# Buffers, marks and begin times in the recurrence of a hybrid block, and four weight loads of its branch stage

## The chip, the cores and the metric

One core of one Trainium2 chip. The metric is the device time of one execution in microseconds. The engines named below are TensorE (PE, with its weight loads PEld), VectorE (DVE), ScalarE (ACT), GpSimd (POOL), and the SyncE queue (SP), which issues most DMAs.

## The reference

One block over 1024 tokens of 1024 channels, all in float32: an input norm and one wide projection, attention with a forget gate (8 heads of 64), an RWKV-7 recurrence (8 heads of 64), a gated sum of the two, an output projection, and a feed-forward net with a short convolution. The change lies in the recurrence and in the gated sum:

```python
def step(state, inp):
    r_t, w_t, k_t, v_t, a_t, b_t = inp
    sa = jnp.einsum('bhvk,bhk->bhv', state, a_t)
    state = state * w_t[:, :, None, :] + sa[..., None] * b_t[:, :, None, :] \
            + v_t[..., None] * k_t[:, :, None, :]
    return state, jnp.einsum('bhvk,bhk->bhv', state, r_t)
...
bonus = (jnp.sum(r_h * k_h * r_k, axis=-1, keepdims=True) * v_h).reshape(bsz, seq, RWKV_WIDTH)
return ((y + bonus) * g).astype(p.dtype)
...
merged = gate_fox * (o_fox @ fox_w_out) + gate_rwkv * (o_rwkv @ rwkv_w_out)
return merged @ w_o
```

## The kernel before

Products with weights are made from split operands: a float32 tile becomes a high part (`hi`) and a rest (`lo`), and three matmuls give one product. The cast to `hi` is done by ACT, the subtraction for `lo` by DVE (L274).

The recurrence runs in chunks of 64 tokens. Its work is cut into eight units, k = 0 to 7: four pairs of heads `p`, each in two halves `hf` of 512 tokens; names such as `cum1_0` or `X0_1` end in p_hf, so `cum1_0` is unit 2. Each unit has a preparation, `pre`, and a main chain, `main`. Three streams are woven together on PE in an order written when the program is built: the main chain of one unit, the preparation of a later one, and as filling the matmuls of the projections (`qk`, `rkv`, `v`, the gates `gt`). The weaver keeps a clock of its own (`weave.now`, in ns) from the costs of the matmuls; a step that yields a number lets that much of filling pass. PE's order is fixed so; on the other engines a scheduler places the instructions, and each engine and each DMA queue works in its order.

The steps that matter here:

- `pre` loads the decay `cum` (L711) and the gains `al` (L713) by SP, scans `cum` on DVE (L715), and ACT makes `el` (L719) and `en` (L721) from it. L732 to L744 form `kr`, `ar`, `bk` and again `al`. PE multiplies `ar` and `bk` into `p`, L764 takes it from PSUM into `E`.
- Corner blocks of `E` go by a store (`sm`, L772) and a load (`M`, L776) into 32-row form; 31 pairs of small DVE operations (L784, L786) invert them; a store and a load (L797) bring the result into `TT`.
- `head_sums` makes the bonus sum `bs`: it splits its operand into two tiles, multiplies both by a block matrix, and L827 uses the sum.
- `main` transposes corners of `TT` into `X` (L842, two instructions), and from `X` come `xi`, `zi`, `TT` again (L859 on ACT) and `uw` on PE, then the chunk states and `y`.
- Tiles of the pool `rw` have one buffer where nothing else is said (`cum`, `al`, `el`, `en`, `kr`), so a load into one waits for the last reader of what is in it.
- A mark with NOSYNC orders two instructions of the same engine without a wait: the one comes behind the other in the queue. L842 has such marks behind the last `S` and the last `E`.
- `ready` (L777) is the time at which a unit's main chain begins, on the weaver's clock. 
- `shifted` empties the bank of a projection: ACT writes `sh` (L366), DVE the result (L369; the `v` of it is the last of a unit). `qk_steps` empties by L393 on ACT and L395 on DVE, and stores both parts with DMAs into `d_st`.

In the branch stage, `br_load` loads the weights of the two gated products, x = 0 for attention and x = 1 for the recurrence, n = 0 to 7, through a tile `raw` with two buffers; ACT casts them (L1219), POOL makes the rest (L1222), and `br_open` loads the gate `g` (L1224). `after_gate` puts an instruction behind the last load of a `g` on SP.

Of the kernel before, what the change touches and what calls it, by code (L numbers as in the profile page):

```python
# [10 lines left out]
F32R = mybir.dt.float32r  # L11
AF = mybir.ActivationFunctionType
ALU = mybir.AluOpType
# [3 lines left out]
S = 1024  # L17
KT = 8
NH = 512
# [113 lines left out]
def hybrid_block(ctx: ExitStack, tc: tile.TileContext, a, out):  # L133
    nc = tc.nc
    weave = Weave()
    ctx.enter_context(tc.manual_schedule(engines={mybir.EngineType.PE}))

    def mm(o, lhsT, rhs, start, stop, more=False):

        weave.mm_cost(o, lhsT, rhs)  # L140
        nc.tensor.matmul(o, lhsT, rhs, start=start, stop=stop, skip_group_check=more)  # L141
# [5 lines left out]
    def f32(ap):  # L147
        return ap.bitcast(F32)

    tt, stt, ts = nc.vector.tensor_tensor, nc.vector.scalar_tensor_tensor, nc.vector.tensor_scalar  # L150
# [15 lines left out]
    def V(name, i=0, n=1):  # L166
        o, _ = VEC[name]
        return vec[:, o + i : o + i + n]
# [13 lines left out]
    omu = cp.tile([128, 14], F32, name="omu")  # L182
# [61 lines left out]
    marks = {}  # L244
# [40 lines left out]
    def gemm_steps(ps, w, x, cs, nk=KT, w0=0, by_kt=False):  # L285
        (wh, wl), (xh, xl) = w, x
        order = [(i, kt) for i in range(3) for kt in range(nk)]
        if by_kt:
            order.sort(key=lambda o: o[1])
        for n, (i, kt) in enumerate(order):  # L290
            ww, xx = ((wh, xh), (wh, xl), (wl, xh))[i]
            k0 = (w0 + kt) * 128
            mm(ps, ww[:, k0 : k0 + 128], xx[:, kt, cs], start=n == 0, stop=n == len(order) - 1)
            yield
# [51 lines left out]
    with ExitStack() as es:  # L346
# [4 lines left out]
        def big(name):  # L351
            return pb.tile([128, NH], F32, tag="big", name=name)

        def gen(name):
            return pr.tile([128, NH], F32, tag="gen", name=name)

        def shifted(w, ti, hf, dst, prev, name, by_kt=False):

            ps = big(f"ps_{name}{hf}")
            yield from gemm_steps(ps, w, u, slice(hf * NH, hf * NH + NH), by_kt=by_kt)  # L360
            sh = shp.tile([128, NH + 1], F32, tag="sh", name=f"sh_{name}{hf}")
            if hf == 0:
                nc.vector.memset(sh[:, 0:1], 0.0)
            else:
                nc.vector.tensor_copy(sh[:, 0:1], prev)
            nc.scalar.activation(sh[:, 1 : NH + 1], ps, AF.Copy, scale=V("mu", ti))  # L366
            if hf == 0:
                nc.gpsimd.tensor_copy(prev, sh[:, NH : NH + 1])
            stt(dst, ps, omu[:, ti : ti + 1], sh[:, 0:NH], op0=ALU.mult, op1=ALU.add)  # L369

        rkv, got, last_col = {}, {}, {}

# [28 lines left out]
        HS = (slice(0, 64), slice(64, 128))  # L401
# [11 lines left out]
        with tc.tile_pool(name="st", bufs=1) as st, tc.tile_pool(name="stp", bufs=2, space=PS) as stp, \  # L413
# [126 lines left out]
            for half in range(2):  # L540
                for kt in u_steps(half):
                    low_part(kt, half, (0, 1))
                    if half == 0 and kt in (3, 5):
                        raw, hi, lo = low_raw[kt == 5]
# [145 lines left out]
        def head_sums(ps, x, hi, lo):  # L690

            nc.scalar.copy(hi, x)
            nc.gpsimd.tensor_tensor(lo, x, f32(hi), op=ALU.subtract)
            yield 3400
            mm(ps, blk_r, hi, start=True, stop=False)
            mm(ps, blk_r, lo, start=False, stop=True)

        def pre(k, p, hf):

            n = f"{p}_{hf}"  # L700
# [3 lines left out]
            def tmp(nm, w=NH, bufs=1, dt=F32):  # L704
                return rw.tile([128, w], dt, tag=nm, name=f"{nm}{n}", bufs=bufs)

            def chunk_tile(nm, bufs, *dims):
                return rw.tile([128, *dims], F32, tag=nm, name=f"{nm}{n}", bufs=bufs)

            cum = tmp("cum")  # L710
            nc.sync.dma_start(cum, d_lora[0, p, :, cs])  # L711
            al = tmp("al")
            nc.sync.dma_start(al, d_lora[1, p, :, cs])  # L713
            for c0 in (0, 256):
                nc.vector.tensor_tensor_scan(cum[:, c0 : c0 + 256], cst2[:, 128:384], cum[:, c0 : c0 + 256], initial=0.0,  # L715
                                             op0=ALU.mult, op1=ALU.add)
# [3 lines left out]
            en = tmp("en")  # L720
# [10 lines left out]
            kr = tmp("kr")  # L731
# [15 lines left out]
            rkb = tmp("ksq")  # L747
# [6 lines left out]
            E = chunk_tile("E", 2, NCU, 2, 3, CH)  # L754
            QA = chunk_tile("QA", 2, NCU, 2, CH)
            UV = chunk_tile("UV", 2, NCU, 2, CH)
            for c0 in range(0, NCU, 4):
                ps = [gen(f"p1_{n}{h}{c0}") for h in range(2)]
# [15 lines left out]
            M32 = chunk_tile("M32", 1, 32, 32)  # L774
            for g in range(4):
                nc.sync.dma_start(M32[g * 32 : g * 32 + 32, :, :], sm.rearrange("h c b s t -> (h c b) s t"))  # L776
            ready = weave.now + (49500 if k == 0 else 38500)  # L777
            E32 = chunk_tile("E32", 1, 8, 32)
            nc.gpsimd.dma_start(E32, a["cst"][:, CST["einit"][0] :].rearrange("p (j t) -> p j t", t=32))
            t32 = tmp("t32", 128)  # L780
# [26 lines left out]
            a4 = at.rearrange("p (b h s) -> p b h s", h=2, s=CH)  # L807
            for e in range(2):
                for h in range(2):
                    nc.scalar.copy(UV[HS[1 - h], e::2, h, :], v4[HS[e], :, h, :])  # L810
                    nc.vector.tensor_copy(QA[HS[h], e::2, 1, :], a4[HS[e], :, h, :])
            yield 2000
            ps = [gen(f"tb{n}{h}") for h in range(2)]
            for c in range(NCU):
# [7 lines left out]
                    mm(q[HS[h], c * CH : c * CH + CH], E[HS[1 - h], c, h, 0, :], UV[HS[1 - h], c, h, :], start=True, stop=True)  # L822
            nc.vector.tensor_copy(QA[:, :, 0, :], c3(q))
            bp = gen(f"bs{n}")
            yield from head_sums(bp, rkb, tmp("cum", dt=F32R), tmp("en", dt=F32R))
            bon = tmp("bon", bufs=2)
            tt(bon, bp, vv, op=ALU.mult)  # L827
            units[p, hf] = dict(ready=ready, pcd=pcd, ar=ar, E=E, QA=QA, TT=TT, bon=bon, UV=UV)
# [1 line left out]
        def main(k, p, hf):  # L830
            o = units.pop((p, hf))
            n = f"{p}_{hf}"
            cs = slice(hf * NH, hf * NH + NH)
            pcd, ar, E, QA, TT, bon, UV = (o[k] for k in ("pcd", "ar", "E", "QA", "TT", "bon", "UV"))
# [5 lines left out]
            yield max(0, o["ready"] - weave.now - 2500)  # L840
            for h in range(2):
                i = nc.vector.transpose(X[B0[h], :, :], TT[B0[h], :, 0:32])  # L842
                for x in ("S", "E"):
                    if x in marks:
                        tc.add_manual_dep(i.ins, marks[x].ins.name, NOSYNC)
            yield max(1300, o["ready"] - weave.now)
# [16 lines left out]
            for c0 in range(0, NCU, 4):  # L863
                ps = gen(f"uw{n}{c0}")
                for c in range(c0, c0 + 4):
                    for h in range(2):
                        x = (c - c0) * 128
# [7 lines left out]
            for c0 in range(0, NCU, 4):  # L875
                ps = gen(f"mz{n}{c0}")
                for c in range(c0, c0 + 4):
                    for h in range(2):
                        x = (c - c0) * 128
# [9 lines left out]
            S = [state.get(p)]  # L889
# [85 lines left out]
        def main_chain():  # L975
            for k, (p, hf) in enumerate(order):
                while (p, hf) not in units:
                    yield 200
                yield from main(k, p, hf)
                yield 0  # L980
# [205 lines left out]
    def bank(k, name):  # L1186
        return pb.tile([128, NH], F32, tag="big", name=name) if k > 5 else pz.tile([128, NH], F32, tag=f"p{k}", name=name)
# [16 lines left out]
    def after_gate(i):  # L1204
        if "g" in marks:
            tc.add_manual_dep(i.ins, marks["g"].ins.name, NOSYNC)

    def br_load(x, n):
        raw = br_raw[x, n] = rp.tile([128, 1024], F32, tag="raw", name=f"raw_br{x}{n}")[:, 0:NH]
        after_gate(nc.sync.dma_start(raw, a["w_br"][n, :, x * NH : x * NH + NH]))  # L1210

    def br_open(x, n):
        if (x, n) not in br_raw:
# [15 lines left out]
    if "rest" in marks:  # L1229
        g, m = (gsp.tile([128, NH], F32, tag="sp0", name=f"rest{k}") for k in range(2))  # L1230
        i = nc.scalar.activation(g, marks["rest"], AF.Abs)
# [89 lines left out]
    for x in range(2):  # L1321
        for n in range(8):
            if x or n:
                k = 8 * x + n + 1
# [320 lines left out]
    ps = {t: [bank(k, f"wo{t}_{c}") for c, k in enumerate(ks)] for t, ks in enumerate(((0, 5), (6, 7), (1, 2)))}  # L1645
# [13 lines left out]
    def wo_do(t, k):  # L1659
        ps = [bank(k + c, f"wo{t}_{c}") for c in range(2)]  # L1660
        for kt in range(KT):
            wo_mm(t, kt, ps)
        return ps

    ps = wo_do(3, 3)
# [7 lines left out]
    ps = wo_do(4, 0)  # L1673
# [15 lines left out]
    for t, k in ((5, 2), (6, 6), (7, 4)):  # L1689
        ps = wo_do(t, k)  # L1690
# [234 lines left out]
    for s, k in enumerate(ORDER):  # L1925
        ps = banks[4:] if k in (7, 4, 2) else banks[0:4]
# [109 lines left out]
```

## Time and profile before

Three runs: median 1654.64 us (1653.51 to 1662.36). The profiled execution took 1657.87 us, its span is 1656.1 us, the mean granted clock of TensorE 0.994. From the profile, by stage (us busy):

| stage | from, to | length | PE | DVE | ACT | POOL | granted clock |
|---|---|---|---|---|---|---|---|
| norm, small projections | 0 to 140 | 140.0 | 127.05 | 98.49 | 76.33 | 12.06 | 0.98 |
| recurrence with projections | 140 to 620 | 480.0 | 467.39 | 344.32 | 231.67 | 62.18 | 1.00 |
| attention | 620 to 827 | 207.0 | 198.81 | 163.81 | 137.21 | 35.40 | 0.99 |
| branches | 827 to 917 | 90.0 | 87.89 | 67.83 | 28.77 | 23.88 | 1.00 |
| output projection | 917 to 1015 | 98.0 | 98.00 | 50.33 | 27.20 | 0.00 | 1.00 |
| feed-forward, up | 1015 to 1438 | 423.0 | 420.65 | 332.12 | 209.82 | 0.00 | 1.00 |
| feed-forward, down | 1438 to 1656.1 | 218.1 | 210.59 | 164.55 | 110.60 | 0.00 | 0.99 |

A row of the timeline gives the start and the length of an instruction in us, its engine and line, output and inputs with their shapes, and in brackets how long the engine was idle before it and what ended that.

### The profile page before, as it was taken

How to read it: one execution, taken by the hardware profiler on the slowest of the kernel's cores; microseconds unless marked ns; L12 is line 12 of the kernel's file. 1: busy time of each engine (PE TensorE's matmuls, PEld its weight loads, DVE VectorE, ACT ScalarE, POOL GpSimd, SP SyncE). 2: the span in 40 equal slices, each digit the busy share in tenths (PEclk: the TensorE clock that was granted, in tenths of full speed). 3: DMA queues.
4: the chain of work that ended last, by engine and by line, in shares of the span. 5: the costliest groups of instructions: out<-in, count | busy, mean ns of one | idle time of the engine just before them, and what ended most of it. 6: DMA issues, size and time to landing. Idle time of an engine off the chain costs nothing.

```text
span 1656.1 us, 25949 instructions
## 1 busy us (share of the span) xinstructions
PE 1610.4 (97%) x9694; PEld 1340.5 (81%) x9694; DVE 1221.4 (74%) x2373; ACT 821.6 (50%) x1537; POOL 133.5 (8%) x153
## 2 busy tenths in 40 slices
PE   7999999999999999999999999999999999999998
PEld 7777777897878788888887888788888888888886
DVE  5786787878876636888778447897777777886677
ACT  5563335445455655666633225644444444555455
POOL 0010101111111011221031000000000000000000
PEclk9999999999999999999999999999999999999999
DMA  9487645443333336434197421243223233674463
GB/s 337 139 322 233 178 122 140 125 122 104 100 115 97 96 114 165 125 105 124 35 358 242 184 85 43 77 134 102 96 97 119 96 99 106 212 264 157 123 210 108
DMA packets 121645, 240.59 MB, mean 145 GB/s; under 512 B 40048, under 2 KB 48880, under 8 KB 121520
## 3 DMA queue, kind: packets, MB, share of 16 engines
q1 hardware_dynamic: 113040, 220.58, 40.8%
q0 software_dynamic: 8480, 18.37, 4.2%
q8 instruction: 76, 1.25, 0.3%
q14 instruction: 49, 0.40, 0.1%
HBM read 173.35 MB, written 65.54 MB: 144 GB/s over the span
## 4 chain that ended last, share of the span: by engine, by line
PE 61%; DVE 5%; ACT 2%; DMA 2%; issue 1%; SPq 0%; POOL 0%; ACTq 0%; DVEq 0%
PE X L141 13%; PE D L141 13%; PE Y L141 6%; PE wo L141 5%; PE gt L141 5%; PE rk_ps L141 4%; PE W L141 3%; PE br L141 3%; PE lg L141 2%; PE ov L141 2%; PE tp L145 2%; PE ps_rkv L141 1%; DMA raw_wo<-in_w_o 1%; DVE nm L1049 1%; DVE P L1059 1%
## 5 line engine op out<-in xcount | busy, mean ns | idle before, releaser
L141 PE MATMUL D<-op,op 128*128 128x512 f32 x924 | 209.8, 389 | 0.0
L141 PEld LDWEIGHTS D<-op,op 128*128 128x128 f32 x924 | 173.4, 188 | 36.2 <-DVE op L1259 0.3
L141 PE MATMUL X<-T_m,S 128*128 128x512 f32 x440 | 107.8, 390 | 1.6 <-ACT T_m L1720 1.1
L141 PEld LDWEIGHTS X<-T_m,S 128*128 128x128 f32 x440 | 82.4, 188 | 20.4 <-ACT T_m L1720 2.5
L1258 ACT CAST op<-g 128x512 fp32r<-128x512 f32 x77 | 47.8, 621 | 73.7 <-PE D L141 48.8
L1259 DVE TENSOR_TENSOR op<-g,op 128x512 fp32r<-128x512 f32 x77 | 53.0, 689 | 41.3 <-ACT op L1258 41.3
L1517 DVE SCALAR_TENSOR_TENSOR c<-ab,vec,c 128x512 f32<-128x512 f32 x88 | 65.9, 750 | 18.4 <-ACT c L1520 16.8
L784 DVE TENSOR_TENSOR t<-E,M 128x60 f32<-128x60 f32 (+24 forms) x248 | 56.5, 228 | 26.5 <-DMA M<-sm 20.5
L274 DVE TENSOR_TENSOR lo_in<-raw_in,hi_in 128x512 fp32r<-128x512 f32 x84 | 57.7, 725 | 20.8 <-PE gt L141 7.2
L1483 DVE TENSOR_TENSOR A<-ur,A 128x512 fp32r<-128x512 f32 x64 | 44.0, 689 | 38.7 <-ACT A L1479 38.5
L1483 DVE TENSOR_TENSOR S<-ur,S 128x512 fp32r<-128x512 f32 x66 | 45.5, 691 | 35.2 <-ACT S L1479 35.1
L1479 ACT CAST S<-ur 128x512 fp32r<-128x512 f32 x66 | 41.0, 622 | 55.8 <-DVE ur L1472 30.6
L141 PE MATMUL Y<-T_h,A 128*128 128x512 f32 x264 | 63.7, 390 | 0.3 <-ACT T_h L1720 0.3
L141 PE MATMUL Y<-T_h,S 128*128 128x512 f32 x264 | 63.6, 390 | 0.4 <-ACT T_h L1738 0.4
L1053 ACT ACTIVATE P<-lg,nm 128x896 f32<-128x896 f32 (+3 forms) x64 | 47.5, 744 | 28.6 <-DVE nm L1049 19.6
L1479 ACT CAST A<-ur 128x512 fp32r<-128x512 f32 x64 | 39.6, 622 | 43.1 <-PE X L141 31.3
L786 DVE TENSOR_TENSOR E<-E,t 128x60 f32<-128x60 f32 (+24 forms) x248 | 55.9, 225 | 6.4
L141 PE MATMUL W<-B_f,A 128*128 128x512 f32 x252 | 60.6, 389 | 0.0
L141 PE MATMUL X<-B_b,A 128*128 128x512 f32 x252 | 60.5, 389 | 0.0
L141 PEld LDWEIGHTS Y<-T_h,S 128*128 128x128 f32 x264 | 49.5, 188 | 11.1 <-ACT T_h L1738 0.8
L141 PEld LDWEIGHTS Y<-T_h,A 128*128 128x128 f32 x264 | 49.5, 188 | 11.0 <-ACT T_h L1720 0.7
L1089 DVE TENSOR_TENSOR tl<-tp,th 128x512 fp32r<-128x512 f32 (+1 forms) x80 | 49.4, 633 | 9.2 <-ACT th L1086 8.5
(483 smaller groups left out, 4132.4 us busy)
## 6 DMA issues: line engine op xcount, KB each, us to landing
raw_in<-in_w_in SPq DMA_DIRECT2D x50, 512.0 KB, 3.9
wm<-in_w_mod SPq DMA_DIRECT2D x48, 512.0 KB, 7.2
ur<-in_w_up SPq DMA_DIRECT2D x44, 512.0 KB, 3.8
g<-d_g SPq DMA_DIRECT2D x35, 512.0 KB, 4.0
d_g<-gs SPq DMA_DIRECT2D x44, 256.0 KB, 2.0
d_g<-c SPq DMA_DIRECT2D x33, 256.0 KB, 4.5
d_st<-qh SPq DMA_DIRECT2D x64, 128.0 KB, 2.4
stA<-d_st POOLq DMA_DIRECT2D x8, 1024.0 KB, 6.7
```

Source lines behind the costliest of these rows:

```text
L141: nc.tensor.matmul(o, lhsT, rhs, start=start, stop=stop, skip_group_check=more)
L145: nc.tensor.transpose(o, i, eye)
L274: nc.vector.tensor_tensor(lo[:, c : c + NH], raw[:, c : c + NH], f32(hi[:, c : c + NH]), op=ALU.subtract)
L784: tt(tv, E32[:, 0:J, s : s + 1].to_broadcast([128, J, W]), M32[:, s : s + 1, s + 1 : 32].to_broadcast([128, J, W]), op=ALU.mult)
L786: tt(E32[:, 0:J, s + 1 : 32], E32[:, 0:J, s + 1 : 32], tv, op=ALU.add)
L1053: nc.scalar.activation(e[:, 0:n], lg[:, 0:n], AF.Exp, bias=nm[:, 0:1], accum_out=nm[:, 1:2])
L1089: tt(tl[:, 0:w], tp[:, 0:w], f32(th[:, 0:w]), op=ALU.subtract)
L1258: nc.scalar.copy(hi, src)
L1259: tt(lo, src, f32(hi), op=ALU.subtract)
L1479: nc.scalar.copy(hi, src)
L1483: tt(lo, src, f32(hi), op=ALU.subtract)
L1517: stt(c, ab[:, x + hf * NH : x + hf * NH + NH], V("conv_w", 22 * x + i), c, op0=ALU.mult, op1=ALU.add)
```

## The change

Four edits: the two parts of the bonus sum are written into the tiles `kr` and `al` instead of `cum` and `en`; the main chains of the units k = 5 to 7 get a later `ready`; the transposes L842 are put, for unit 0, behind the last bank emptied by L369 (`bank`) and, for k = 5 to 7, behind the last copy into `QA`; and the branch weights with x = 1 are no longer put behind a load of `g`.

```diff
@@ shifted
-            stt(dst, ps, omu[:, ti : ti + 1], sh[:, 0:NH], op0=ALU.mult, op1=ALU.add)
+            marks["bank"] = stt(dst, ps, omu[:, ti : ti + 1], sh[:, 0:NH], op0=ALU.mult, op1=ALU.add)
@@ pre
-            ready = weave.now + (49500 if k == 0 else 38500)
+            ready = weave.now + (49500 if k == 0 else 38500 if k < 5 else 41000)
...
-                    nc.vector.tensor_copy(QA[HS[h], e::2, 1, :], a4[HS[e], :, h, :])
+                    marks["QA"] = nc.vector.tensor_copy(QA[HS[h], e::2, 1, :], a4[HS[e], :, h, :])
...
-            yield from head_sums(bp, rkb, tmp("cum", dt=F32R), tmp("en", dt=F32R))
+            yield from head_sums(bp, rkb, tmp("kr", dt=F32R), tmp("al", dt=F32R))
@@ main
-                for x in ("S", "E"):
+                for x in ("S", "E", "bank") if k == 0 else ("S", "E", "QA") if k > 4 else ("S", "E"):
@@ br_load
-        after_gate(nc.sync.dma_start(raw, a["w_br"][n, :, x * NH : x * NH + NH]))
+        i = nc.sync.dma_start(raw, a["w_br"][n, :, x * NH : x * NH + NH])
+        if x == 0:
+            after_gate(i)
```

With `cum` and `en` free earlier, the scheduler puts the load, the scan and the two exponentials of the next unit about one unit earlier. DVE in unit 0's preparation, before:

```order
L741 TENSOR_TENSOR ar0_0_1333<-r00_637,el0_0_1240 128x512
L395 SCALAR_TENSOR_TENSOR ql4_0_1295<-qk4_0_1268,qh4_0_1293 128x512
L274 TENSOR_TENSOR lo_in5_1365<-raw_in5_1362,hi_in5_1364 128x512 x2
L732 SCALAR_TENSOR_TENSOR kr0_0_1330<-ksq0_0_1327,k00_638 128x512
L395 SCALAR_TENSOR_TENSOR ql4_1_1354<-qk4_1_1303,qh4_1_1352 128x512
L737 SCALAR_TENSOR_TENSOR ar0_0_1333<-kr0_0_1330,nkk_86,el0_0_1240 128x512
L738 SCALAR_TENSOR_TENSOR kr0_0_1330<-kr0_0_1330,vec_72,al0_0_1236 128x512
L739 TENSOR_TENSOR bk0_0_1332<-kr0_0_1330,en0_0_1243 128x8x64
```

The same place on DVE after the change:

```order
L741 TENSOR_TENSOR ar0_0_1333<-r00_637,el0_0_1240 128x512
L395 SCALAR_TENSOR_TENSOR ql4_0_1295<-qk4_0_1268,qh4_0_1293 128x512
L715 SCALAR_TENSOR_TENSOR cum0_1_1685<-cst2_120,cum0_1_1685 128x256 x2
L274 TENSOR_TENSOR lo_in5_1365<-raw_in5_1362,hi_in5_1364 128x512 x2
L732 SCALAR_TENSOR_TENSOR kr0_0_1330<-ksq0_0_1327,k00_638 128x512
L395 SCALAR_TENSOR_TENSOR ql4_1_1354<-qk4_1_1303,qh4_1_1352 128x512
L737 SCALAR_TENSOR_TENSOR ar0_0_1333<-kr0_0_1330,nkk_86,el0_0_1240 128x512
L738 SCALAR_TENSOR_TENSOR kr0_0_1330<-kr0_0_1330,vec_72,al0_0_1236 128x512
L741 TENSOR_TENSOR ar0_1_1750<-r01_640,el0_1_1691 128x512
L739 TENSOR_TENSOR bk0_0_1332<-kr0_0_1330,en0_0_1243 128x8x64
```

Unit 1's scan and L741 stand here now; before, they stood some 40 rows later, in unit 1. Likewise unit 2's scan now stands between unit 0's two pairs of L764, and unit 6's, unit 7's and the others a unit earlier; on SP the load of `cum` stands where that of `al` stood, and the other way round. On ACT, where unit 1's main chain is (`TT0_1`), before:

```order
L852 COPY X0_1_2755<-xi0_1_2784 32x256 x2
L393 ACTIVATE qh3_1_2810<-qk3_1_2728 128x512
L719 ACTIVATE el1_1_2771<-cum1_1_2765 128x8x64
L721 ACTIVATE en1_1_2774<-cum1_1_2765 128x512
L859 COPY TT0_1_1986<-zi0_1_2836 32x8x32 x2
```

The same place on ACT after the change:

```order
L852 COPY X0_1_2755<-xi0_1_2784 32x256 x2
L393 ACTIVATE qh3_1_2810<-qk3_1_2728 128x512
L859 COPY TT0_1_1986<-zi0_1_2836 32x8x32 x2
L729 ACTIVATE ksq1_1_2859<-ssq1_1_2803,epsr_76 128x512
L730 ACTIVATE ksq1_1_2859<-ksq1_1_2859 128x512
```

The two exponentials of unit 3 are gone from ahead of L859. DVE around unit 0's transposes, before:

```order
L827 TENSOR_TENSOR bon0_1_2096<-bs0_1_2073,v01_642 128x512
L842 STREAM_TRANSPOSE X0_0_1684<-TT0_0_1572 32x256
L274 TENSOR_TENSOR lo_in17_2113<-raw_in17_2110,hi_in17_2112 128x512 x2
L842 STREAM_TRANSPOSE X0_0_1684<-TT0_0_1572 32x256
L369 SCALAR_TENSOR_TENSOR v10_1683<-ps_rkv90_2030,omu_80,sh_rkv90_2105 128x512
L784 TENSOR_TENSOR t320_1_1918<-E320_1_1916,M320_1_1911 128x31
L715 SCALAR_TENSOR_TENSOR cum1_0_2119<-cst2_120,cum1_0_2119 128x256 x2
```

The same place on DVE after the change:

```order
L827 TENSOR_TENSOR bon0_1_2096<-bs0_1_2073,v01_642 128x512
L274 TENSOR_TENSOR lo_in17_2113<-raw_in17_2110,hi_in17_2112 128x512 x2
L369 SCALAR_TENSOR_TENSOR v10_1683<-ps_rkv90_2030,omu_80,sh_rkv90_2105 128x512
L842 STREAM_TRANSPOSE X0_0_1684<-TT0_0_1572 32x256 x2
L784 TENSOR_TENSOR t320_1_1918<-E320_1_1916,M320_1_1911 128x31
```

L369 and the L274 of the `hi_in17` weights now come ahead of both transposes, and the scan is gone from here. In the other units the order around L842 stays but for unit 5, where the second transpose comes ahead of one operation. PE's order changes in unit 7 alone: its main chain comes 12 matmuls later. On SP, `raw_br17` now stands ahead of `g1_5` instead of behind `g1_6`, and the loads before it have moved up likewise.

## The prediction

> **What bounds the kernel now.** The page comes first, then the waits of PE.
>
> ```profile
> PE 1610.4 (97%) x9694; PEld 1340.5 (81%) x9694; DVE 1221.4 (74%) x2373; ACT 821.6 (50%) x1537; POOL 133.5 (8%) x153
> PE qk L141 <- DVE v L369: 2.8, 1, 2.8
> ```
>
> PE is busy for 1610.4 of 1656.1 us, so all that any reordering can win is some 46 us of PE idle time, and the change touches only a few of those waits. It adds and removes no matmul. The question is therefore which single waits go, and which new ones come. The list of PE's waits has 1.7 to 2.8 us each for three of them, here the longest; I read the timelines around each.
>
> First wait, unit 0 (DVE, then PE):
>
> ```profile
> 216.75 0.68 DVE L827 TENSOR_TENSOR bon<-bs,v 128x512 f32<-128x512 f32 x1
> 222.50 0.43 DVE L842 STREAM_TRANSPOSE X<-TT 32x256 f32<-32x256 f32 x1 [5.07 <-DMA TT<-se]
> 222.87 1.24 DVE L274 TENSOR_TENSOR lo_in<-raw_in,hi_in 128x512 fp32r<-128x512 f32 x2
> 224.15 0.43 DVE L842 STREAM_TRANSPOSE X<-TT 32x256 f32<-32x256 f32 x1
> 224.61 0.75 DVE L369 SCALAR_TENSOR_TENSOR v<-ps_rkv,omu,sh_rkv 128x512 f32<-128x512 f32 x1
> 225.42 2.12 PE L141 MATMUL qk<-u_hi,hi_in 128*128 128x512 f32 x8 [2.78 <-DVE v L369]
> 227.92 0.25 PE L141 MATMUL xi<-X,E 32*32 32x32 f32 x4
> 216.79 0.69 ACT L366 ACTIVATE sh_rkv<-ps_rkv,vec 128x512 f32<-128x512 f32 x1 [1.30 <-PE ps_rkv L141]
> ```
>
> DVE stands 5.07 us at a transpose whose DMA has not landed, and behind it waits L369, which empties the PSUM bank that PE needs. PE loses 2.78 us. The input of L369 was there at 216.79+0.69 = 217.48.
>
> Second wait, unit 1 (DVE, ACT, PE, then one slice of the windows view: PE busy, weight loads, DVE, ACT, POOL, granted clock, DMA share, GB/s):
>
> ```profile
> 281.78 1.27 DVE L715 TENSOR_TENSOR_SCAN cum<-cst,cum 128x256 f32<-128x256 f32 x2 [1.32 <-DMA cum<-d_lora]
> 283.09 0.63 ACT L719 ACTIVATE el<-cum 128x512 f32<-128x512 f32 x1 [3.66 <-DVE cum L715]
> 284.14 0.73 ACT L859 COPY TT<-zi 32x256 f32<-32x256 f32 x2
> 284.54 3.37 PE L141 MATMUL uw<-QA,TT 64*64 64x128 f32 x32 [1.73 <-ACT TT L859]
> 285.68:289.10 3.42, 3.42 (x25) 2.90 (x20) 3.35 (x11) 1.31 (x4) 0.61 (x2) 0.50 0.82 280
> ```
>
> ACT stands 3.66 us at L719, waiting for the scan of the next unit's decay, which waits for its DMA. The copy L859 that PE needs is queued behind it. PE loses 1.73 us, and the 3.42 us behind that run at a granted clock of 0.50, another 1.71 us. The Trainium skill (TensorE: Matmul & The Clock Gate, Part 1) says the clock halves after an idle window of about 3.4 us. By it a gap of 1.73 us would not do so; this row differs.
>
> The same ACT queue costs PE once more in unit 5, and the fourth wait is in the branch stage (SP, POOL, ACT, PE, and the summary of line L1210):
>
> ```profile
> 480.44 0.63 ACT L719 ACTIVATE el<-cum 128x512 f32<-128x512 f32 x1 [0.81 <-DVE cum L715]
> 482.42 1.81 PE L141 MATMUL uw<-QA,TT 64*64 64x128 f32 x24 [0.84 <-ACT TT L859]
> 906.74 0.38 SPq L1210 DMA_DIRECT2D raw_br<-in_w_br  x1
> 898.57 1.45 POOL L1222 TENSOR_TENSOR lo_br<-raw_br,hi_br 128x512 fp32r<-128x512 f32 x1 [5.04 <-ACT hi_br L1219]
> 911.21 0.62 ACT L1219 CAST hi_br<-raw_br 128x512 fp32r<-128x512 f32 x1 [1.93 <-DMA raw_br<-in_w_br]
> 911.88 0.98 PE L141 MATMUL br<-rk_m,hi_br 128*128 128x512 f32 x3 [2.11 <-ACT hi_br L1219]
> DMA to landing us min/median/max: 3.7/4.8/8.7
> ```
>
> The last weight of the branch stage is issued only at 906.74, because a `g` load stands ahead of it on SP.
>
> **The change part by part.** *Transposes (k=0).* L369 goes ahead of both transposes and can run at about 217.5, long before PE wants the bank at 222.64. The 2.78 go. Next late would be xi, which moves up to 227.92−2.78 = 225.1; its transposes would end near 224.6, so nothing is late. −2.8. For k above 4 the mark only moves one 0.43 transpose past one DVE operation at which PE has no wait: 0.
>
> *Bonus parts into `kr` and `al`.* The next unit's `cum` load, scan, L719 and L721 go a whole unit earlier, `al` goes later. So in unit 1 and unit 5 nothing stands ahead of L859 but what PE itself feeds: −1.73 −1.71 −0.84 = −4.3. The bill comes in units 0 and 1, where the scan is now put between instructions that others wait for:
>
> ```profile
> 151.16 0.62 ACT L721 ACTIVATE en<-cum 128x512 f32<-128x512 f32 x1
> 149.31 1.27 DVE L715 TENSOR_TENSOR_SCAN cum<-cst,cum 128x256 f32<-128x256 f32 x2 [5.65 <-DMA cum<-d_lora]
> 144.87 0.54 SPq L711 DMA_DIRECT2D cum<-d_lora  x1
> 157.81 0.69 DVE L395 SCALAR_TENSOR_TENSOR ql<-qk,qh 128x512 fp32r<-128x512 f32 x1 [2.63 <-DMA d_st<-ql]
> 162.88 0.69 DVE L395 SCALAR_TENSOR_TENSOR ql<-qk,qh 128x512 fp32r<-128x512 f32 x1 [0.95 <-DMA d_st<-ql]
> 163.49 0.68 DVE L744 TENSOR_TENSOR bk<-al,en 128x512 f32<-128x512 f32 x1
> 164.22 1.16 PE L141 MATMUL p<-ar,bk 64*128 64x128 f32 x16 [0.82 <-DVE bk L744]
> DMA to landing us min/median/max: 2.5/3.0/3.5
> ```
>
> (The last row is the summary of L711, the `cum` loads.) The load for unit 1 can start when L721 has read the old `cum`, 151.16+0.62 = 151.8. It lands 2.5 to 3.5 us later, or 4.4 as the load before it took (144.87 to the scan at 149.31): 154.3 to 156.2. The scan (1.27), the two L274 (1.2) and L732 (0.7) follow, so the next L395 starts at 157.5 to 159.4 instead of 157.81. Its 2.63 us of waiting covered most of it; what is left is 0 to 1.6, and I take 1.0, nearer to the slow load, which was issued only 7 us before. L744 and with it PE's `p` at 164.22 are late by that 1.0. The added L741 (0.6) fits into the 0.95 us of idle time ahead of the L395 behind it.
>
> ```profile
> 167.37 0.53 SPq L713 DMA_DIRECT2D al<-d_lora  x1
> 166.62 1.40 DVE L274 TENSOR_TENSOR lo_in<-raw_in,hi_in 128x512 fp32r<-128x512 f32 x2
> 169.49 0.69 DVE L395 SCALAR_TENSOR_TENSOR ql<-qk,qh 128x512 fp32r<-128x512 f32 x1 [1.46 <-DMA d_st<-qh]
> 170.09 1.28 DVE L764 TENSOR_TENSOR E<-p,cst 128x512 f32<-128x512 f32 x2
> 181.89 0.19 DVE L784 TENSOR_TENSOR t<-E,M 128x31 f32<-128x31 f32 x1 [6.29 <-DMA M<-sm]
> 188.57 1.66 PE L141 MATMUL qk<-u_hi,hi_in 128*128 128x512 f32 x6 [0.57 <-DVE ql L395]
> ```
>
> Unit 2's `cum` load takes the place that `al` had on SP at 167.37, and needs the new L721, which must wait for L744. It is issued at 167.4 to 168.4 and lands at 169.9 to 171.9. DVE stands at the scan meanwhile, and behind it are L274, L395 and the second pair of L764: 1.27+1.3+0.6+1.28 = 4.45 from the landing, so that pair ends at 174.4 to 176.4, where it ended at 171.37. That is 3.0 to 5.0 late, and 5.5 if a load takes the 4.4 of above; I take 4.0. From that pair goes a chain without slack: the `sm` store, the `M` load, L784 at 181.89 (DVE stood 6.29 for it), and among these small operations the L395 that PE waited for at 188.57. PE is thus 4.0 late there, the 1.0 of above included. It then stands about 3.6 us in one piece, longer than the 1.73 that halved the clock in unit 1: another 1.7. Bounds for the clock: 0 and 3.4 (two windows). Sum: +5.7, from +3.0 to +8.9.
>
> In the later units the scan comes shortly before the end of a chain of L784 and L786, which gives `TT`, and waits up to 1.3 (the row at 281.78) for a load. `TT` and the transposes are late by as much, and DVE holds what stands behind them. Xi itself has room, as in unit 2:
>
> ```profile
> 315.58 0.44 DVE L842 STREAM_TRANSPOSE X<-TT 32x256 f32<-32x256 f32 x1 [0.30 <-DMA TT<-se]
> 327.57 0.76 ACT L852 COPY X<-xi 32x256 f32<-32x256 f32 x2 [0.25 <-PE xi L141]
> ```
>
> These are 12.0 us apart. The last scan, in unit 5's preparation, stands ahead of L764. I put 0.5 for all of them, from 0 to +2.5 (twice 1.3). Nothing below zero: the waits of PE that I haven't named have other releasers than a scan.
>
> *Later `ready`.* Only the last unit's order moves: its main chain starts 12 matmuls later, which are filled by gate matmuls from behind.
>
> ```profile
> 621.19 1.98 PE L141 MATMUL gt<-u_hi,lo_in 128*128 128x512 f32 x8
> ```
>
> Twelve of these are at most 12×1.98/8 = 3.0 us. PE works on, since gate matmuls are left until 621.19+1.98 = 623.2; that cover gone, it would cost up to 3.0. 0.
>
> *Branch loads.* Without the mark, `raw_br17` goes ahead of `g1_5` and waits only for a free buffer, that is for L1222 at 898.57+1.45 = 900.0. With 3.7 to 8.7 it lands at 904 to 909, and PE wants it cast at 909.77: −2.1, at the worst −1.5. `g1_5`, now behind it, can be issued at 900.4 and lands at 905.2 with the 4.8 of that row; DVE needs it for the L1316 at 906.22:
>
> ```profile
> 906.22 0.67 DVE L1316 TENSOR_TENSOR g<-g,br 128x512 f32<-128x512 f32 x1
> ```
>
> So that hides, with 1 us to spare; beyond it, each further us holds back a bank and costs up to 1.
>
> The sum: −2.8 −4.3 +5.7 +0.5 −2.1 = −3.0 against the profiled execution of 1657.87 us. That one is 3.2 above the median of the runs, 1654.64, so I expect 1651.6 there. By the skill's rule the halved window of unit 1 would not come back as a gain, while the gap of 3.6 would still cost one: the sum would be −1.3.
>
> **The rivals.** *Full gain.* The early loads land before DVE gets there, or the chain behind L764 has slack that I don't see. Then −2.8−4.3−2.1 = −9.2: 1645.4. For it: DVE idles 2.63, 0.95 and 1.46 us in just those rows, room for waits. Against: 6.29 us at L784 with the chain of stores ahead, which is no room. 0.22.
>
> *Slower: the scan blocks DVE.* If unit 2's load is kept back on SP behind the stores of `qh` and lands near 177 rather than 171, the second L764 ends at 181.5, ten us late; PE stands that long, with two windows at half clock: 10+3.4−9.2 = +4, that is 1659, and another 4 where the last scan does the same to the L764 behind it. It decides at a landing of 173.9: 173.9+4.45−171.37 = 7.0 late, which with 1.7 of clock and the 0.5 of the later units eats the 9.2. The loads of L711 were never that slow, but those of L1210 took up to 8.7. 0.17.
>
> *The clock goes by the skill's page.* A rule of long idle windows as a mechanism here: the 0.50 after 284.54 belongs to the free-running window in which it fell and comes back somewhere else. Then 1.7 of the gain is missing: 1653.3. Against it, the clock fell just behind that gap. 0.08.
>
> *The early loads don't come.* If `raw_br17` and the transposes find another wait in the same place (SP's own queue, `hi_in` for the L274 ahead of L369), 4.9 are missing, −3.0+4.9 = +1.9, and the kernel is at 1656.5. 0.08.
>
> **How the numbers follow.** My forecast, part of the gain given back in unit 1, has 0.45, with 1648 to 1655 from the bounds +3.0 and +8.9. The range reaches from 1644.5, just below the full gain, to 1659.5, the first size of the slower case. This kernel's runs tell 0.5% (8.3 us) from no change, so faster means below 1646.4 and slower above 1662.9. Faster: most of the full gain's 0.22, since it lands right at that line, 0.18. Slower: the part of the blocked DVE in which the last scan adds its share, 0.08. Same: 0.74.
>
> **What would show it.** Right: no PE wait on L369 near 225, none on L859 near 284, the clock whole behind it, no wait on `hi_br` at 911; a PE wait of 3 to 4 us on L395 near 190, the clock at 0.50 behind it, the first L784 near 186. Wrong: that L784 still near 182 (full gain), or beyond 190 (slower); a new PE wait in units 2 to 7 that is over 2 us.

## The result and the profile after

The changed kernel takes 1648.95 us (median of 6 runs, 1646.33 to 1649.31) against 1657.53 us (6 runs, 1653.51 to 1662.36): ratio 0.9945 with a 95% interval of 0.9933 to 0.9957, some 9 us. The time lies inside the range, but the gain is close to the 9.2 us of the rival "full gain" and not to the 3.0 of the forecast; that it meets the rival's size is luck, as the section on the prediction works out. The profiled execution took 1648.91 us, its span is 1647.1 us.

The page's row of busy times, and the first rows of the list of PE's waits that stand behind the start of the kernel:

```profile
PE 1607.8 (98%) x9694; PEld 1339.6 (81%) x9694; DVE 1222.6 (74%) x2373; ACT 820.9 (50%) x1537; POOL 130.8 (8%) x153
PE rk_ps L141 <- ACT gm L1163: 3.1, 3, 1.9
PE sp L141 <- ACT S L903: 2.8, 4, 1.4
PE qk L141 <- DVE ql L395: 2.3, 1, 2.3
```

The wait for L369, the one for L859 and the one for `hi_br` have left the top of the list; the one for L395 has grown. The matmuls of both kernels stand in the same order up to unit 7, so the start of the same matmul in both traces tells where time was won (us):

| matmul | before | after | difference | since the row above |
|---|---|---|---|---|
| `p`, unit 0 | 164.22 | 163.13 | −1.09 | −1.09 |
| `qk` behind L395 | 188.57 | 189.22 | +0.65 | +1.74 |
| `qk` behind L369 | 225.42 | 224.62 | −0.80 | −1.45 |
| `uw`, unit 1 | 284.54 | 281.18 | −3.36 | −2.56 |
| `v` behind L955 | 447.66 | 440.72 | −6.94 | −3.58 |
| `uw`, unit 5 | 482.42 | 474.76 | −7.66 | −0.72 |
| `rk_ps` | 629.78 | 622.39 | −7.39 | +0.27 |
| `br`, last weights | 911.88 | 903.04 | −8.84 | −1.45 |

Some rows hold two things. The first −1.09 comes from a load that landed earlier in this run, ahead of anything that the change touches. The −1.45 behind L369 is −2.9 at that matmul and +1.5 for matmuls that ran at half clock behind 189 us. The last −1.45 is −2.2 at the last weights, +0.6 at the first of the branch stage, and a half clock that follows a wait near 622 after the change (+1.6) and one near 680 before it (−1.4).

The first gains, in the timelines of DVE, ACT and PE:

```profile
220.16 0.74 DVE L369 SCALAR_TENSOR_TENSOR v<-ps_rkv,omu,sh_rkv 128x512 f32<-128x512 f32 x1
221.62 0.43 DVE L842 STREAM_TRANSPOSE X<-TT 32x256 f32<-32x256 f32 x1 [0.71 <-DMA TT<-se]
224.62 1.99 PE L141 MATMUL qk<-u_hi,hi_in 128*128 128x512 f32 x8
278.80 0.75 ACT L859 COPY TT<-zi 32x256 f32<-32x256 f32 x2 [1.03 <-PE zi L141]
281.18 1.96 PE L141 MATMUL uw<-QA,TT 64*64 64x128 f32 x32
903.04 1.98 PE L141 MATMUL br<-rk_m,hi_br 128*128 128x512 f32 x8
```

None of the three PE rows has a wait in brackets any more. L859 now waits for PE's `zi` alone and ends 1.6 us before `uw`. The bill in units 0 and 1, in the timelines of DVE, SP (its DMA queue) and PE, and in two slices of the windows view:

```profile
153.50 1.28 DVE L715 TENSOR_TENSOR_SCAN cum<-cst,cum 128x256 f32<-128x256 f32 x2 [1.57 <-DMA cum<-d_lora]
162.40 0.68 DVE L744 TENSOR_TENSOR bk<-al,en 128x512 f32<-128x512 f32 x1
168.92 1.28 DVE L715 TENSOR_TENSOR_SCAN cum<-cst,cum 128x256 f32<-128x256 f32 x2 [3.31 <-DMA cum<-d_lora]
171.90 1.28 DVE L764 TENSOR_TENSOR E<-p,cst 128x512 f32<-128x512 f32 x2
173.19 2.27 SPq L772 DMA_DIRECT2D sm<-E  x4
182.54 0.19 DVE L784 TENSOR_TENSOR t<-E,M 128x31 f32<-128x31 f32 x1 [6.66 <-DMA M<-sm]
189.22 1.05 PE L141 MATMUL qk<-u_hi,hi_in 128*128 128x512 f32 x2 [2.31 <-DVE ql L395]
186.04:189.45 3.41, 1.10 (x5) 0.60 (x4) 3.33 (x10) 1.06 (x3) 0.00 (x0) 1.00 0.54 137
189.45:192.87 3.42, 3.42 (x9) 2.67 (x9) 3.04 (x13) 0.40 (x1) 0.00 (x0) 0.50 0.64 144
```

The mechanism of the forecast is there: DVE stands at both early scans, PE waits at L395, and the clock is halved behind it. Two waits are new or gone that no part of the prediction named. Near 297 ACT holds PE up, since L721 must wait for L744 (`en` has one buffer) and a chunk state stands behind it:

```profile
296.47 0.63 ACT L721 ACTIVATE en<-cum 128x512 f32<-128x512 f32 x1 [0.21 <-DVE bk L744]
297.36 0.43 PE L141 MATMUL sp<-S,Mt 128*128 128x64 f32 x2 [1.38 <-ACT S L903]
```

And the 1.42 us that PE waited for `vs` at 447.66 before are gone:

```profile
433.54 0.69 DVE L715 TENSOR_TENSOR_SCAN cum<-cst,cum 128x256 f32<-128x256 f32 x1 [0.76 <-DMA cum<-d_lora]
447.66 1.21 PE L141 MATMUL v<-hi_v,u_hi 128*128 128x256 f32 x8 [1.42 <-DVE vs L955]
```

This wait is 1.28 and 1.74 in the kernels without the bonus edit further down and below 0.5 in those with it. That the scan at 433.54, which stood on DVE before, was what made `vs` late is argued, not shown.

### The profile page after: what moved, and what is told of

The parts are those of the page before. It is cut to its first block, busy times and chain, and to the rows that moved or that the text cites. A ratio compares the mean times of both kernels' runs of the same rounds, so it can differ in the third digit from the quotient of the medians.

```text
span 1647.1 us, 25947 instructions
## 1 busy us (share of the span) xinstructions
PE 1607.8 (98%) x9694; PEld 1339.6 (81%) x9694; DVE 1222.6 (74%) x2373; ACT 820.9 (50%) x1537; POOL 130.8 (8%) x153
## 4 chain that ended last, share of the span: by engine, by line
PE 58%; DVE 5%; ACT 2%; DMA 2%; issue 1%; SPq 0%; ACTq 0%; DVEq 0%
PE X L141 13%; PE D L141 13%; PE Y L141 6%; PE wo L141 5%; PE br L141 4%; PE rk_ps L141 3%; PE W L141 3%; PE gt L141 3%; PE lg L141 2%; PE ov L141 2%; PE tp L145 2%; DMA d_gate<-gs 1%; DVE nm L1049 1%; DVE P L1059 1%; DVE tl L1089 0%
## 5 line engine op out<-in xcount | busy, mean ns | idle before, releaser
L784 DVE TENSOR_TENSOR t<-E,M 128x60 f32<-128x60 f32 (+24 forms) x248 | 55.6, 224 | 27.9 <-DMA M<-sm 21.8
L274 DVE TENSOR_TENSOR lo_in<-raw_in,hi_in 128x512 fp32r<-128x512 f32 x84 | 56.7, 712 | 17.6 <-PE gt L141 4.8
L272 ACT CAST hi_in<-raw_in 128x1024 fp32r<-128x1024 f32 x42 | 43.8, 1048 | 26.3 <-PE ps_rkv L141 11.3
```

What stands on the lines that cost most here:

```text
L272: nc.scalar.copy(hi, raw)
L274: nc.vector.tensor_tensor(lo[:, c : c + NH], raw[:, c : c + NH], f32(hi[:, c : c + NH]), op=ALU.subtract)
L784: tt(tv, E32[:, 0:J, s : s + 1].to_broadcast([128, J, W]), M32[:, s : s + 1, s + 1 : 32].to_broadcast([128, J, W]), op=ALU.mult)
```

## The experiments

Each ratio is to the kernel before, run on the same chip beside it. Its median there was 1656.17 to 1657.53 us, so two medians from different chips can differ by a microsecond or so for that alone; each interval reaches some 2 us to either side. The changed kernel was measured twice, with 0.9945 and 0.9951.

| kernel | median us | ratio, 95% interval |
|---|---|---|
| changed kernel | 1648.95 | 0.9945 (0.9933 to 0.9957) |
| without the bonus edit | 1654.77 | 0.9998 (0.9988 to 1.0008) |
| without the `bank` mark | 1649.75 | 0.9961 (0.9949 to 0.9973) |
| without the branch loads | 1651.10 | 0.9969 (0.9958 to 0.9980) |
| without the later `ready` | 1648.96 | 0.9952 (0.9939 to 0.9965) |
| bonus edit from unit 1 on | 1651.52 | 0.9962 (0.9948 to 0.9976) |
| bonus edit from unit 2 on | 1652.36 | 0.9972 (0.9956 to 0.9987) |
| before, `bank` mark alone | 1660.05 | 1.0013 (1.0001 to 1.0025) |
| before, bonus edit alone | 1655.11 | 0.9986 (0.9974 to 0.9998) |
| changed kernel again | 1650.14 | 0.9951 (0.9939 to 0.9964) |
| without the `QA` mark | 1649.12 | 0.9953 (0.9941 to 0.9965) |
| one scan put later | 1645.09 | 0.9929 (0.9917 to 0.9941) |
| and one L721 put later | 1647.91 | 0.9945 (0.9930 to 0.9961) |

**One edit undone.** First the bonus edit:

```diff
-            yield from head_sums(bp, rkb, tmp("kr", dt=F32R), tmp("al", dt=F32R))
+            yield from head_sums(bp, rkb, tmp("cum", dt=F32R), tmp("en", dt=F32R))
```

> The changed kernel with the bonus parts back in cum and en (early scans gone, the other three edits kept). Theory A (matching the two traces matmul by matmul: the early el and en are worth 1.9+2.0 us in unit 1 with its half clock, 0.8 in unit 5 and 1.4 at the vs wait of 447; the early scans cost 1.7 in units 0 and 1, another 1.7 of half clock behind it, and 1.5 at the chunk states near 297): about 4 us of PE's gaps come back against 5 that go, so this kernel is 1 to 4 us slower than the changed one, 1650 to 1653; PE's wait before L395 near 189 is below 1 us, the clock behind it whole, and the wait before uw near 282 is back with 1.5 to 2. Rival B (the edit is the bulk of the gain): 6 to 8 us slower, 1655 to 1657. Rival C (the bill in units 0 to 2 is as large as the gain): same time within 1 us.

It is 5.8 us slower than the changed kernel in the median and some 8 us by the ratios; theory A gave 1 to 4, rival B 6 to 8. In the timelines of this kernel:

```profile
228.31 1.27 DVE L715 TENSOR_TENSOR_SCAN cum<-cst,cum 128x256 f32<-128x256 f32 x2 [2.98 <-DMA cum<-d_lora]
229.61 0.63 ACT L719 ACTIVATE el<-cum 128x512 f32<-128x512 f32 x1 [11.98 <-DVE cum L715]
232.37 0.75 ACT L852 COPY X<-xi 32x256 f32<-32x256 f32 x2
232.78 1.45 PE L141 MATMUL zi<-TT,X 32*32 32x32 f32 x32 [4.16 <-ACT X L852]
```

The wait that the mark takes away at 225 comes back seven us later: unit 2's scan still stands behind the transposes, ACT waits for it ahead of the copy of `xi`, and PE loses 4.16 us at `zi`, with two windows at half clock behind it. No theory had this wait. Next, the mark, the branch loads and `ready`:

```diff
-                for x in ("S", "E", "bank") if k == 0 else ("S", "E", "QA") if k > 4 else ("S", "E"):
+                for x in ("S", "E") if k == 0 else ("S", "E", "QA") if k > 4 else ("S", "E"):
```

> The changed kernel with unit 0's transposes marked as before (no bank mark). Theory A: L369 waits behind the first transpose again and PE loses 2.8 to 3.0 us at 225, so 1651.5 to 1652, perhaps 1.7 more if a half clock follows that gap. Rival B: since PE is late by the scans in units 0 and 1, the TT load lands early enough by PE's clock and only 1 us is lost, 1650.

```diff
-        if x == 0:
-            after_gate(i)
+        after_gate(i)
```

> The changed kernel with all branch weights behind a load of g as before. Theory A: raw_br17 is issued only after g1_6 and PE waits 2.1 at the cast of it near 903, and the wait of 0.35 near 837 goes: 1.8 us slower, 1650.8. Rival B: g loads that now come late cost as much elsewhere, no difference.

```diff
-            ready = weave.now + (49500 if k == 0 else 38500 if k < 5 else 41000)
+            ready = weave.now + (49500 if k == 0 else 38500)
```

> The changed kernel with ready at 38500 for all later units. Theory A: the later main chain of unit 7 puts its store d_orw on SP ahead of a gate store, ACT's L337 waits 4.6 us for that store near 613, and PE's wait before rk_ps near 622 grows from 1.2 to 1.9 with a half clock behind it (1.7): without the edit the wait is 1.2 or less, and the time 0.8 to 2.5 us shorter, 1646.5 to 1648.2. Rival B: the edit costs nothing and the grown wait is chance: the same within 0.5 us. Rival C: the edit pays in unit 7 (its transposes wait for TT): 1 to 2 us slower without it.

PE's rows, one of each kernel in this order, with a second one of the first kernel:

```profile
190.86 1.42 PE L141 MATMUL qk<-u_hi,hi_in 128*128 128x512 f32 x5 [1.89 <-DVE ql L395]
227.66 1.65 PE L141 MATMUL qk<-u_hi,hi_in 128*128 128x512 f32 x6 [2.31 <-DVE v L369]
```

```profile
904.48 1.21 PE L141 MATMUL br<-rk_m,hi_br 128*128 128x512 f32 x4 [1.90 <-ACT hi_br L1220]
```

```profile
624.10 1.19 PE L141 MATMUL rk_ps<-u_hi,hi_in 128*128 128x512 f32 x4 [1.18 <-ACT gm L1163]
```

Without the mark PE waits 2.31 for L369, as theory A had it, but the time doesn't settle it: 0.8 us longer in the median, 1.7 to 2.6 by the ratios, with intervals that overlap. Its profiled execution had no half clock behind 189 (the wait of 1.89 fell into two windows) and a `rk_ps` wait of 1.18; both go the other way. The branch loads are worth 2.1 us in the median, 3 to 4 by the ratios, and the wait of 1.90 is there: theory A. The later `ready` shows no worth, the same median and 0.9952: rival B. The larger `rk_ps` wait of the changed kernel's profile is not its doing, since the kernels without the mark and without the branch loads have the later `ready` and 1.18 there.

**Where the scans stand, and the edits alone.** In `pre`, the two tiles chosen by unit; `k < 2` in the second kernel:

```diff
-            yield from head_sums(bp, rkb, tmp("kr", dt=F32R), tmp("al", dt=F32R))
+            two = ("cum", "en") if k == 0 else ("kr", "al")
+            yield from head_sums(bp, rkb, tmp(two[0], dt=F32R), tmp(two[1], dt=F32R))
```

> The changed kernel, but unit 0 keeps its bonus parts in cum and en, so the early scans of units 1 and 2 are not put between unit 0's L395 and L764; unit 2's scan comes in unit 0's chain of L784 and L786 instead. Theory A (the early scans in unit 0 cost 1.7 us of waiting at 189 and often 1.7 of half clock): that wait falls below 0.7 and the time by 1.7 to 3.4, to 1645.5 to 1647.2. Rival B (a load that is asked for late makes DVE stand wherever the scan is put): the load for unit 2, issued near 191, holds up the chain, TT comes 1 to 3 us later and PE waits for xi or zi near 228; no gain, 1648 to 1650.

> The changed kernel, but units 0 and 1 keep their bonus parts in cum and en: unit 2's scan stands behind unit 0's transposes as before the change. Theory A (the transposes' mark gains only if that scan is gone from behind them): ACT waits for the scan ahead of the copy of xi, PE waits 2 to 4 us for zi near 230, often with a half clock, and the early gain of 1.7 at 189 is paid back: 1648.5 to 1652. Rival B (mark and scans are independent): as with unit 0 alone undone, 1645.5 to 1647.2.

The wait at 189 falls to 0.66 in the first of them, yet it is 2.6 slower in the median (1.8 to 2.8 by the ratios). Both halves of unit 2's scan now stand in unit 1's own work on DVE, at 196.59 and 197.83, ahead of the L744 that PE waits for in the first row:

```profile
202.53 1.14 PE L141 MATMUL p<-ar,bk 64*128 64x128 f32 x15 [1.67 <-DVE bk L744]
253.69 0.86 PE L141 MATMUL ps_rkv<-u_hi,hi_in 128*128 128x512 f32 x2 [1.68 <-DVE k L369]
```

What makes L369 late in the second row isn't shown; the changed kernel waits 0.73 us for it in its second profile. Rival B was nearer on the time and wrong on the place (xi, zi). In the second kernel unit 2's scan stands behind the transposes again, and PE waits for `zi`, as theory A had it:

```profile
229.22 1.07 PE L141 MATMUL zi<-TT,X 32*32 32x32 f32 x32 [1.84 <-ACT X L853]
```

Then the kernel before with one edit each: the mark `bank` set and used for k = 0, or the bonus parts in `kr` and `al`, and nothing else of the change.

> The kernel before with one edit: unit 0's transposes behind the last L369. Theory A: the wait of 2.8 before qk at 225 goes, but zi then waits some 4 us for ACT, which stands at L719 for unit 2's scan; 0 to 2 us slower than before, 1655.5 to 1658. Rival B (the term as in the prediction): 2.8 faster, 1653.5.

> The kernel before with one edit: the bonus parts in kr and al. Theory A (the sum of the runs so far: what the three other edits bring together with it is 0.8 for the mark, 2.1 for the branch loads, 0 for ready): 2.9 slower than the changed kernel, 1651.5 to 1652.5, some 4 faster than before; the wait before qk at 225 is there with 2.3 to 2.8. Rival B (it needs the mark to pay): within 1.5 us of before.

The mark alone makes the kernel slower, 1.0013 (1.0001 to 1.0025): theory A. PE and two slices of the windows view:

```profile
229.89 1.34 PE L141 MATMUL zi<-TT,X 32*32 32x32 f32 x29 [2.08 <-ACT X L852]
230.09:233.50 3.41, 3.27 (x37) 2.75 (x36) 3.03 (x13) 2.11 (x5) 0.00 (x0) 0.50 0.89 205
233.50:236.92 3.42, 3.42 (x16) 2.41 (x16) 3.16 (x10) 0.39 (x1) 0.00 (x0) 0.50 0.61 140
```

The wait for `zi` is 2.08 us, where theory A had some 4. The bonus edit alone brings 2 us, half of what theory A had and little more than the 1.5 of rival B. It has the wait for L369 (2.38 us), and another one in unit 5, where the transposes now wait for `TT` ahead of the copies into `QA`:

```profile
462.75 0.43 DVE L842 STREAM_TRANSPOSE X<-TT 32x256 f32<-32x256 f32 x1 [5.58 <-DMA TT<-se]
464.95 1.95 PE L141 MATMUL q<-UV,E 64*64 64x64 f32 x32 [2.55 <-DVE QA L811]
```

Alone the two edits are worth +0.1% and −0.1%; together (the kernel without the branch loads, which also has the `QA` mark and the later `ready`) 0.9969, 5 us. The bonus edit takes away the wait for `zi` that the mark uncovers. The wait for `QA` that the bonus edit uncovers goes by a third edit, the `QA` mark.

**The QA mark and the early scan of unit 2.** The changed kernel once more, and without the `QA` mark:

> The changed kernel once more, as the measure for the three beside it: 1648 to 1650. Its waits at 189 (2 to 3 us before L395) and near 297 (1.4 before the chunk states) are there again; the half clock behind 189 follows only if at least 1.7 us of that wait fall into one of the 3.41 us windows.

Both waits are there again, 2.04 us at 189 and 1.39 near 297. The first is split by the edge of a window into 1.58 and 0.46, and the clock stays whole behind it, as expected.

```diff
-                for x in ("S", "E", "bank") if k == 0 else ("S", "E", "QA") if k > 4 else ("S", "E"):
+                for x in ("S", "E", "bank") if k == 0 else ("S", "E"):
```

> The changed kernel without the QA mark of the units 5 to 7. Theory A (as in the kernel with the bonus edit alone, where unit 5's transposes wait 5.6 us for TT ahead of the QA copies, PE then 2.55 us for QA, and a half clock follows): 2.5 to 4.2 us slower than the changed kernel, 1651.5 to 1653. Rival B (the term as in the prediction, 0): 1648 to 1650, no PE wait on QA near 460.

```profile
462.06 1.15 PE L141 MATMUL q<-UV,E 64*64 64x64 f32 x32 [2.66 <-DVE QA L811]
```

The wait of theory A is there, the time is not: 1649.12 against 1650.14. Two waits of the changed kernel that come right behind (0.85 at 466 and 0.76 at 473 in its second profile) are gone in exchange. What the `QA` mark is worth stays below what these runs resolve.

The changed kernel's second profile is the longest of its five runs, 1656.45, and shows one reason why runs of one kernel spread:

```profile
623.71 0.60 ACT L337 ACTIVATE gs<-gt 128x512 f32<-128x512 f32 x1 [9.06 <-DMA d_gate<-gs]
628.04 1.22 PE L141 MATMUL rk_ps<-u_hi,hi_in 128*128 128x512 f32 x2 [6.34 <-ACT gm L1163]
```

ACT waits 9.06 us for the store of a gate tile (4.64 in the first profile, 2.97 in the kernel before), and PE 6.34. What keeps that store was not tried.

The last two kernels put single instructions elsewhere. In `pre`:

```diff
+                if k == 2:
+                    tc.add_manual_dep(i.ins, marks["E", k - 2].ins.name, NOSYNC)
```

with `i` the scan and `marks["E", k]` the last L764 of unit k. On DVE only unit 2's scan moves, from between unit 0's two pairs of L764 to behind the second.

> The changed kernel with one instruction moved: unit 2's scan stands behind unit 0's second pair of L764 instead of between the pairs. Theory A (the scan's wait for its load delays L395, L764, the sm store and the L395 before 189): that wait of PE falls from 2.3 to 1.0 or less, no half clock behind it, 1.3 to 3.4 us faster than the changed kernel, 1645.5 to 1647.5. Rival B (the chain from L764 has slack, and the wait at 189 comes from the M load and the stores on SP): less than 0.7 us faster.

This is the fastest kernel of all: 1645.09 against 1650.14 for the changed kernel beside it, 0.9929 (0.9917 to 0.9941) of the kernel before. On DVE (two lines are numbered higher by two or three here, L764 is L766 and L784 is L787) and on PE:

```profile
168.38 1.28 DVE L766 TENSOR_TENSOR E<-p,cst 128x512 f32<-128x512 f32 x2
169.57 1.26 DVE L715 TENSOR_TENSOR_SCAN cum<-cst,cum 128x256 f32<-128x256 f32 x2
180.13 0.19 DVE L787 TENSOR_TENSOR t<-E,M 128x31 f32<-128x31 f32 x1 [5.86 <-DMA M<-sm]
186.81 2.11 PE L141 MATMUL qk<-u_hi,hi_in 128*128 128x512 f32 x8
```

The load has landed when DVE comes to the scan, the pair ends 3.5 us earlier, the `M` load 2.4, and PE's row has no wait of 0.45 or more. This is theory A, and its mechanism is shown by one moved instruction. All the profiles bear it out: PE's wait before this L395 is 1.89 to 3.12 us in the seven in which unit 2's scan stands between the pairs, and below 1 us in the seven in which it doesn't. The gain over the changed kernel beside it is 3.6 us by the ratios and 5.1 in the medians, more than the 1.3 to 3.4 of theory A; the runs beside it include the long one with the wait for the gate store. The second adds, for L721 of unit 4, a mark behind the first chunk state of unit 1:

```diff
+            if k == 4:
+                tc.add_manual_dep(i.ins, marks["S", 1, 0].ins.name, NOSYNC)
```

> The same kernel, and unit 4's L721 is put behind the first chunk state of unit 1's main chain on ACT. Theory A (L721 waits for L744 because en has one buffer, and PE's chunk state stands behind it, 1.38 us near 297): that wait goes, another 1.0 to 1.4 us faster, 1644.5 to 1646.5. Rival B (the next instruction in ACT's order takes its place, or the later L721 delays unit 5's load and scan and with them its chain): no faster than the kernel with the scan alone.

```profile
295.60 0.43 PE L141 MATMUL sp<-S,Mt 128*128 128x64 f32 x2 [0.55 <-ACT S L908]
625.23 2.08 PE L141 MATMUL rk_ps<-u_hi,hi_in 128*128 128x512 f32 x4 [5.72 <-ACT gm L1168]
```

The wait near 297 falls from 1.38 to 0.55, but its runs lie in two groups, three at 1645.1 to 1645.2 and three at 1650.6 to 1651.9, and the profile of the longest has the gate store's wait. Whether the edit helps can't be told from these six.

## Why the prediction was right in its range and wrong in its likeliest case

*The wins came as sized, but not one by one.* By the starts of the same matmuls in both traces they are 2.9 at L369, 1.7 at `uw` of unit 1 and 2.0 over the matmuls right behind it, which had been at half clock, 0.7 in unit 5 and 2.2 at the last branch weights (forecast: 2.8, 1.7, 1.7, 0.8 and 2.1). The step "next late would be xi" was wrong by itself: alone, the mark uncovers a wait for `zi` of 2.1 to 4.2 us, as ACT stands at L719 ahead of the copy of `xi`. It held only since the bonus edit takes that scan away. The prediction summed the edits as if each met the trace of before.

*The term that was mis-sized is the bill of units 0 and 1.* Forecast +5.7 (4.0 and 1.7 of clock), measured +1.74 and 1.5 of clock in the first profile, 3.2 together; behind 189 the clock stays whole in the changed kernel's second profile and in the kernel without the mark. Three parts of it: unit 1's load was issued in unit 0 at 150.74 and its scan began at 153.50, and DVE's idle time covered that wholly, so L744 was not late (0 instead of 1.0; the kernels stand 1.06 us apart already at the first scan, 149.31 and 148.25, whose load landed earlier in this run, and 1.09 at L744). Unit 2's scan began at 168.92, which with these 1.1 us is 170.0, the lower bound of the forecast for its load. And the chain behind L764 was not without slack: from the pair's end to L784 it took 10.5 us before and 9.4 after, since in the kernel before SP still issued stores of `qh` ahead of the `sm` store. The reason given against the full gain, "no room", was wrong by that difference of 1.2 (10.52 less 9.36).

*The later units* came out as 0 in sum (+0.5 forecast), with +1.4 near 297 and −1.4 at 447, of which neither was named: the first is a wait on ACT, not on DVE, for the new place of L721 behind L744. "The waits of PE that I haven't named have other releasers than a scan" does not cover the second, which goes with the bonus edit.

*The size of the gain is in part luck.* The profiled executions differ by 9.0 us, 6.0 more than forecast. The bill explains 2.5 of these, the later units 0.5, the wins 0.3, and 1.1 is the chance of the first load. The remaining 1.5 or so are small steps and half-clock windows behind waits that no edit was meant to touch, and they stay unexplained. "Full gain" had no bill at all, so its 9.2 is met by a sum of other terms. Where the bill of unit 2 does go, in the kernel with the one scan put later, the gain is some 12 us.

*Of the rivals*, "slower: the scan blocks DVE" has the right place and a third of its size: by the clock of the kernel before the second pair ended 2.9 us late, not ten. The first L784 came at 182.5, where 190 was that rival's mark and "near 182" the sign of the full gain; but PE did wait at L395, as the forecast had it. "The early loads don't come" fell: `raw_br17` is issued at 890.99. The rival of the half clock fell in its mechanism, as the last part shows, since each halved window has a wait of its own ahead of it. In number it was not far off: between 140 and 1640 us both profiles have two halved windows, from 285.68 and 681.63 on before the change, from 189.45 and 622.95 on after it. `ready` costs nothing that the runs resolve, as forecast; that the `QA` mark is worth 0 was right in time as far as they resolve it, and wrong in reason, since the mark does take away a wait of 2.66 us.

## What to carry to other kernels

An order mark, or a freed buffer, moves a wait to what stands next in an engine's queue; follow the next two users on each engine before a gain is booked, and cost edits that touch the same stretch together. An instruction that waits for a DMA belongs behind the work that others wait for, not between: moving one scan behind two copies (L764) lowered the ratio from 0.9951 to 0.9929, where the whole change had brought it from 1 to 0.9951. For effects of 2 us, compare single waits matmul by matmul, since run to run the halved clock and one slow store move the time by more.

## What the runs showed of the hardware

In these traces the granted clock halves for whole windows of 3.41 us, mostly one, on a grid that is fixed within a trace, and mostly behind a window in which PE idled for about half of the time. In the windows of the kernel before, on that grid, with PE's busy time as the second number:

```profile
220.83:224.24 3.41, 1.80 (x8) 1.13 (x6) 1.70 (x4) 0.00 (x0) 0.76 (x2) 1.00 0.69 170
224.24:227.65 3.41, 2.23 (x10) 1.80 (x10) 2.94 (x9) 0.51 (x1) 0.00 (x0) 1.00 0.73 214
227.65:231.07 3.42, 3.42 (x45) 2.69 (x44) 3.08 (x14) 3.35 (x8) 0.19 (x1) 1.00 0.19 45
282.27:285.68 3.41, 1.68 (x19) 1.06 (x19) 3.41 (x8) 2.51 (x6) 0.51 (x1) 1.00 0.47 90
```

The gap of 2.78 us splits into 1.61 and 1.18, and no window is halved; the gap of 1.73 us falls into one window, and the next, quoted in the prediction, is at 0.50. In the changed kernel a wait of 1.98 at 675.88 splits into 0.23 and 1.74 and does nothing, while the kernel before has the same wait, 1.98 at 681.64, in one window and a halved one behind it. By PE's busy time the limit is not sharp. In all fourteen profiles, from 140 us on, each window with 1.92 us of idle time or more was followed by a halved one. From 1.58 to 1.80 us both are found: halved behind 1.58 at 228.26 us (bonus edit from unit 2 on) and behind 1.73 here, whole behind 1.74 at 674.14 us (changed kernel). Three profiles have a halved window near 1042 us behind one with only 1.1 us of idle time. And a second halved window can follow a first in which PE was busy, as in the kernel with the mark alone, with 3.27 us busy in the window at 230.09. So the idle time of a window is a sign, but not all that the clock goes by; what else does stays open.

The Trainium skill (TensorE: Matmul & The Clock Gate, Part 1) has the window of 3413 ns and that it runs freely. The traces agree: the halved windows of the changed kernel at 189.45 and 622.95 are 433.50 us apart, 127 windows of 3.413 us, and the grid lies elsewhere in another run. The Trainium skill asks there for an idle window of about 3.4 us. Here about half of one did it in most cases, 1.73 us in the last row above.

Since the grid's place differs from run to run, nearly the same wait can cost 1.5 to 1.7 us in one run and nothing in the next: at 189 the changed kernel had a wait of 2.31 us with a halved window behind it in its first profile, and one of 2.04 us without in its second.
